# Padding two SBUF tiles so that matmul operands start at multiples of 512 bytes

## The chip, the cores and the metric

One Trainium2 chip, of which the program uses one core. The metric is the device time of one execution in microseconds (us); the figure before is the median of three runs. The engines are called as the profile calls them: PE (TensorE, the matmuls) and PEld (its weight loads, which can run beside its matmuls), DVE (VectorE), ACT (ScalarE), POOL (GpSimd), SP (SyncE, which issues nearly all transfers).

## The reference, cut to what matters

A decoder trunk of two layers on 256 tokens of width 1024, all in float32. Layer 0 mixes tokens by causal averages over 2, 4, 8 and 16 tokens; layer 1 is sparse attention with 16 heads of 64. Behind each mixer stand a gated FFN with a causal convolution of width 3, and a gated embedding:

```python
def conv_ffn(h, w_up, conv_w, conv_b, w_down):      # h 256 x 1024, w_up 1024 x 5632, w_down 2816 x 1024
    u = h @ w_up
    up = jnp.pad(u, ((0, 0), (CONV_W - 1, 0), (0, 0)))
    u = sum(conv_w[j] * up[:, j:j + S] for j in range(CONV_W)) + conv_b
    a, g = u[..., :D_FF], u[..., D_FF:]
    return (jax.nn.silu(g) * a) @ w_down
...
    x = x + conv_ffn(rmsnorm(x, norm_ffn[i]), ffn_up[i], ffn_conv[i], ffn_conv_b[i], ffn_down[i])
    gate = jax.nn.sigmoid(rmsnorm(x, norm_ple[i]) @ ple_gate[i])
    x = x + gate * (p[i] @ ple_proj[i])
```

## The kernel before, in words

The activations lie transposed in SBUF: 128 partitions (features) by 256 tokens, eight such blocks in the tile `x`. Every product is made exact enough by splitting both operands into a rounded part and a rest of type fp32r (`wh`, `wl` for a weight tile, `dh`, `dl` for a down weight, `xs` for both parts of the activations, `ah`, `al` for the FFN's inner activations). `mm3` (line 101) makes three matmuls of 256 columns: high by high, high weight by low activation, low weight by high activation. `mm2` (line 105), used for the up product alone, makes two: the high weight against both parts of the activations side by side (512 columns), then the low weight against the high part (256 columns).

`ahead` (line 137) prepares weights: SP loads 1 MB into `raw`, ACT copies it to `wh`, DVE subtracts to get `wl`, each in two halves (lines 147 and 149). `down_weights` (line 159) does the same for the down weights.

`ffn` (line 325) runs 22 steps per layer. In step i PE makes the up product (`product`, 2 halves by 8 blocks, so 16 calls of `mm2`, line 338), `evac` (line 369) takes it through a copy, an addition, the norm's row, the convolution (lines 377 to 379, on the tile `un`), silu and the split into `ah`, `al`, and `down` (line 389) multiplies the result of two steps before by its down weights: 8 calls of `mm3`, 24 matmuls. The order on PE is: up product of step i, then down product of step i-2. `gates` (line 456) makes the gate's products by `mm3`; `attention_layer` (line 532) makes keys and values from the split `ks` (1280 columns of them by `mm3`), queries from `qs`, scores from `qq` and `kk`, and the output projection from `xo`.

The tiles lie in SBUF in the order in which their pools are opened and their names first used, each at the next multiple of 32 bytes of a partition. This is what the program of the kernel before has (first buffer of each name; all further buffers of the FFN's weights and activations have the same remainder, as their sizes are multiples of 512 bytes):

| tile | byte in the partition | remainder by 512 | role in the matmuls |
|---|---|---|---|
| cols (748 columns, 2,992 bytes) | 16512 | 128 | per-feature constants, identity (48) |
| x | 19520 | 64 | none (input of the splits) |
| identb, maskb (bf16) | 27712, 27968 | 64, 320 | weights, moving operand (attention's mask) |
| raw | 30912 | 192 | none (loaded weights) |
| wh, wl | 55488, 88256 | 192 | weights; moving operand for the values |
| xs, ks, qs, xo, kk (one slot) | 121024 | 192 | moving operand; ks also weights |
| un0, un1, un2 (2 x 258 columns each) | 159360, 161440, 163520 | 128, 160, 192 | none |
| ub, t1, sg | 165600 on | 224 | none |
| ah, al | 173792, 177888 | 224 | moving operand |
| dh, dl | 190176, 198368 | 224 | weights |
| qq, pe (attention) | 159360, 176256 | 128 | weights (scores, transposes) |
| pt, pc, vz (attention) | 212160, 210112, 205504 | 192 | moving operand, weights |

The lines the change touches are these two; each of the three `un` tiles holds two halves of 2 + 256 columns:

```python
    cols = const.tile([P, NCOL], F32, name="cols")                                            # line 171
...
            uns = [fp.tile([P, 2, T + 2], F32, name=f"un{i}", bufs=1) for i in range(3)]      # line 980
            for u in uns:
                G.memset(u[:, :, 0:2], 0.0)
```

and these are the matmuls that the prediction counts:

```python
    def mm3(o, w, x, first, last):
        for i, (a, b) in enumerate(((0, 0), (0, 1), (1, 0))):
            mm(o, w[a], x[b], first and i == 0, last and i == 2)
    def mm2(o, w, x, first, last):
        mm(o, w[0], x, first, False)
        mm(o[:, 1], w[1], x[:, 0], False, last)
```

Of the kernel before, what the change touches and what calls it, by code (L numbers as in the profile page):

```python
# [10 lines left out]
F32 = mybir.dt.float32  # L11
# [7 lines left out]
P = 128  # L19
T = 256  # L20
# [44 lines left out]
def _columns():  # L65
    at, n = {}, 0
    for name, w in (("mix0", 8), ("pscale", 8), ("ffn0", 8), ("ones", 1), ("invf", 1), ("valid", 2),
                    ("ple0", 8), ("kv", 8), ("mix1", 8), ("ffn1", 8), ("ple1", 8),
                    ("final", 8), ("posk", 16), ("posv", 16), ("ident", 128),
                    ("mask", 160), ("conv0", 176), ("conv1", 176)):  # L70
        at[name] = (n, n + w)
        n += w
    return at, n


COLS, NCOL = _columns()


def body(ctx, tc, xt, xT, pT, pos, colsd, band, wpool, wup, wdn, wgate, wproj, wkv, wq, wqg, wout,
# [3 lines left out]
    const = ctx.enter_context(tc.tile_pool(name="const", bufs=1))  # L83
# [84 lines left out]
        dmade[n] = (hi, lo)  # L168


    cols = const.tile([P, NCOL], F32, name="cols")
    c0, c1 = COLS["ones"][0], COLS["conv0"][0]
    x = const.tile([P, KT, T], F32, name="x")
    pool_ctx = ctx.enter_context(ExitStack())
# [255 lines left out]
    def ple(layer):  # L430
        fp = fpool[0]
        pp, wide, wj, ph, pl = {}, [], [], [], []

        def mixin():

            wj[:] = take()
            ahead(3)
            pj = fp.tile([P, 2, T], F32, name="pj", tag="pj", bufs=1)
            nc.sync.dma_start(pj, pT[:, layer])
            ph[:] = [fp.tile([P, 2, T], F32R, name="ph", tag="ph", bufs=1)]  # L440
            pl[:] = [fp.tile([P, 2, T], F32R, name="pl", tag="pl", bufs=1)]
            S.activation(ph[0], pj, AF.Copy, scale=0.5)
            V.scalar_tensor_tensor(pl[0], pj, 0.5, ph[0].bitcast(F32), op0=ALU.mult, op1=ALU.subtract)
            for m in range(PRE):
                inject(m, 5)

        def inject(m, bk, hs=(0, 1)):
            b = bank(bk)
            for h in hs:
                for k in range(2):  # L450
                    mm3(b[:, h], at(wj, slice(None), k, slice((2 * m + h) * P, (2 * m + h + 1) * P)),
                        (ph[0][:, k], pl[0][:, k]), k == 0, k == 1)
            if len(hs) < 2:
                pp[2 * m + hs[0]] = b[:, hs[0]:hs[0] + 1]
                return
            if m % 2 == 0:
                t = fp.tile([P, D], F32, name="pp", tag="draw", bufs=2)
                wide.append(t.rearrange("p (k t) -> p k t", k=4))
            t = wide[m // 2][:, m % 2 * 2:m % 2 * 2 + 2]
            S.copy(t, b)  # L460
            pp[2 * m], pp[2 * m + 1] = t, t[:, 1:]

        return mixin, lambda: gates(layer, inject, pp)
# [499 lines left out]
    def x0ready(k):  # L963
        b = bank((0, 1, 2, 3, 7, 0, 1, 2)[k], (P, T))
        for i in range(2):
            kk = k - k % 2 + i
            mm(b, wpl[:, kk, (k % 2) * P:(k % 2) * P + P], us[:, kk], i == 0, i == 1)
        V.scalar_tensor_tensor(x[:, k], b, col("pscale", k), x[:, k], op0=ALU.mult, op1=ALU.add)

    for layer in range(2):  # L970
        if layer == 1:
            with tc.tile_pool(name="ap", bufs=2) as ap:
                attention_layer(ap)
        if layer == 0:
            for k in range(KT):
                x0ready(k)
            pool_ctx.close()
        with tc.tile_pool(name=f"fp{layer}", bufs=2) as fp:
            fpool[:] = [fp]
            uns = [fp.tile([P, 2, T + 2], F32, name=f"un{i}", bufs=1) for i in range(3)]  # L980
            for u in uns:
                G.memset(u[:, :, 0:2], 0.0)
            mixin, after = ple(layer)
            ffn(layer, mixin)
            after()
# [138 lines left out]
```

## Time and profile before

| | us |
|---|---|
| median of 3 runs (626.06 to 629.3) | 627.59 |
| the profiled execution | 630.54 |
| its span, first to last instruction | 628.8 |
| PE busy | 606.5 (96%), 4134 matmuls |
| PEld busy | 550.7 (88%), 4134 loads |
| DVE busy | 535.1 (85%) |
| ACT busy | 405.7 (65%) |
| mean granted TensorE clock | 0.981 |

[...]

### The profile page before, as it was taken

Reading aid. Unit: us, or ns where it says so; the run is one execution under the profiler, and the core shown is the slowest. Engines: PE = TensorE matmul, PEld = TensorE weight load, DVE = VectorE, ACT = ScalarE, POOL = GpSimd, SP = SyncE. Lnnn points to the kernel's source line nnn. Section 1 sums busy time; section 2 is a strip of 40 time slices with the busy share of each in tenths; the row PEclk is TensorE's granted clock in tenths of the full one; section 3 lists DMA queues with packets and bytes.
Section 4 is the critical chain, followed back from the end, with each engine's and each line's share of the span. In section 5 each row is a group of like instructions: output and inputs, shape, how many; then the busy total and the mean of one; then the engine's idle time right before and its main releaser. Section 6 shows DMA issues by size and latency. Waiting matters only on the chain.

```text
span 628.8 us, 10871 instructions
## 1 busy us (share of the span) xinstructions
PE 606.5 (96%) x4134; PEld 550.7 (88%) x4134; DVE 535.1 (85%) x981; ACT 405.7 (65%) x777; POOL 47.7 (8%) x69
## 2 busy tenths in 40 slices
PE   7999999999999999999889999899999999999995
PEld 7789999999999999999866677699999999999995
DVE  3999999999988889476988974999999998889853
ACT  4868766666676757463675752786666667666743
POOL 1510000000000323000000000500000000000221
PEclk9999999999999999999968999999999999999999
DMA  8775567654554145855532114255654445552001
GB/s 333 292 263 201 176 225 254 239 212 175 169 193 151 52 151 200 323 182 161 172 105 92 67 38 164 86 201 206 241 207 180 173 179 189 201 201 101 1 2 67
DMA packets 24116, 107.32 MB, mean 171 GB/s; under 512 B 3584, under 2 KB 7680, under 8 KB 15744
## 3 DMA queue, kind: packets, MB, share of 16 engines
q1 hardware_dynamic: 23776, 105.58, 47.0%
q10 hardware_dynamic: 288, 1.05, 0.4%
q8 instruction: 32, 0.52, 0.3%
q14 instruction: 20, 0.16, 0.1%
HBM read 101.80 MB, written 1.05 MB: 164 GB/s over the span
## 4 chain that ended last, share of the span: by engine, by line
PE 82%; DVE 4%; ACT 3%; issue 2%; DMA 1%; SPq 1%; POOL 1%; POOLq 0%; DVEq 0%; ACTq 0%
PE bank L99 80%; PE bank L820 2%; ACT wh L147 1%; DMA draw<-in_wdn 1%; DVE wl L149 1%; POOL sqa L276 0%; DVE dl L167 0%; DVE pt L826 0%; SPq L592 0%; ACT pe L782 0%; DMA kk<-kp 0%; DVE nm L770 0%; SPq L701 0%; ACT xs L227 0%; DVE x L739 0%
## 5 line engine op out<-in xcount | busy, mean ns | idle before, releaser
L99 PE MATMUL bank<-xs,wh 128*128 128x512 f32 (+1 forms) x960 | 296.2, 366 | 3.2 <-DVE xs L228 3.0
L99 PE MATMUL bank<-xs,wl 128*128 128x256 f32 x832 | 234.1, 282 | 0.6 <-DVE wl L149 0.6
L99 PEld LDWEIGHTS bank<-xs,wh 128*128 128x128 f32 x960 | 172.5, 189 | 32.6 <-DVE xs L228 5.3
L149 DVE TENSOR_TENSOR wl<-raw,wh 128x1024 fp32r<-128x1024 f32 (+2 forms) x142 | 166.6, 1183 | 20.5 <-ACT wh L147 20.5
L147 ACT CAST wh<-raw 128x1024 fp32r<-128x1024 f32 (+2 forms) x144 | 141.5, 1006 | 38.7 <-PE bank L99 30.0
L99 PEld LDWEIGHTS bank<-xs,wl 128*128 128x128 f32 x832 | 158.2, 190 | 1.4 <-DVE wl L149 1.3
L99 PE MATMUL bank<-al,dh 128*128 128x256 f32 x352 | 99.3, 283 | 0.0
L99 PE MATMUL bank<-ah,dl 128*128 128x256 f32 x352 | 99.1, 283 | 0.0
L99 PE MATMUL bank<-ah,dh 128*128 128x256 f32 x352 | 98.5, 284 | 0.3
L99 PEld LDWEIGHTS bank<-ah,dh 128*128 128x128 f32 x352 | 66.4, 190 | 2.4 <-ACT ah L386 0.7
L99 PEld LDWEIGHTS bank<-al,dh 128*128 128x128 f32 x352 | 67.4, 191 | 0.0
L99 PEld LDWEIGHTS bank<-ah,dl 128*128 128x128 f32 x352 | 67.2, 191 | 0.0
L276 POOL TENSOR_TENSOR sqa<-sqa,sq 128x256 f32<-128x256 f32 x35 | 31.3, 895 | 397.0 <-issue 370.3
L166 ACT CAST dh<-draw 128x1024 fp32r<-128x1024 f32 x44 | 46.2, 1052 | 20.0 <-PE bank L99 16.4
L377 ACT ACTIVATE t<-un,cols 128x256 f32<-128x256 f32 x88 | 52.3, 601 | 10.2 <-DVE un L373 10.0
L371 ACT COPY ub<-bank 128x256 f32<-128x256 f32 x88 | 32.0, 367 | 39.6 <-PE bank L99 39.6
L167 DVE TENSOR_TENSOR dl<-draw,dh 128x1024 fp32r<-128x1024 f32 x44 | 54.1, 1230 | 0.0
L378 DVE SCALAR_TENSOR_TENSOR t<-un,cols,t 128x256 f32<-128x256 f32 x88 | 42.0, 481 | 5.8 <-ACT t L377 5.5
L379 DVE SCALAR_TENSOR_TENSOR t<-un,cols,t 128x256 f32<-128x256 f32 x88 | 41.9, 481 | 1.7
L372 DVE TENSOR_TENSOR ub<-bank,ub 128x256 f32<-128x256 f32 x88 | 36.3, 418 | 0.5
L373 DVE TENSOR_TENSOR un<-ub,rrow 128x256 f32<-128x256 f32 x88 | 36.4, 419 | 0.3
L386 ACT CAST ah<-sg 128x256 fp32r<-128x256 f32 x44 | 17.8, 404 | 17.3 <-DVE sg L383 17.3
(196 smaller groups left out, 861.9 us busy)
## 6 DMA issues: line engine op xcount, KB each, us to landing
raw<-in_wup SPq DMA_DIRECT2D x44, 1024.0 KB, 4.9
draw<-in_wdn SPq DMA_DIRECT2D x44, 512.0 KB, 4.9
raw<-in_wgate SPq DMA_DIRECT2D x8, 1024.0 KB, 4.8
raw<-in_wkv SPq DMA_DIRECT2D x8, 768.0 KB, 4.4
raw<-in_wq SPq DMA_DIRECT2D x4, 1024.0 KB, 5.1
raw<-in_wout SPq DMA_DIRECT2D x4, 1024.0 KB, 4.9
raw<-in_wproj SPq DMA_DIRECT2D x2, 1024.0 KB, 4.8
w<-in_cw SPq DMA_DIRECT2D x2, 1024.0 KB, 6.2
```

The costliest lines, as they stand in the source:

```text
L99: E.matmul(o, w, x, start=first, stop=last, skip_group_check=True)
L147: S.copy(hi[:, sl], raw[:, sl])
L149: e.tensor_tensor(lo[:, sl], raw[:, sl], hi[:, sl].bitcast(F32), op=ALU.subtract)
L166: S.copy(hi, raw)
L167: V.tensor_sub(lo, raw, hi.bitcast(F32))
L276: G.tensor_tensor(acc, acc, t, op=ALU.add)
L371: S.copy(ub, up[i][h][:, 1])
L372: V.tensor_tensor(ub, up[i][h][:, 0], ub, op=ALU.add)
L373: V.tensor_tensor(un[:, h, 2:], ub, row, op=ALU.mult)
L377: S.activation(t1, un[:, h, 2:], AF.Identity, scale=c[2], bias=c[3])
L378: V.scalar_tensor_tensor(t1, un[:, h, 1:T + 1], c[1], t1, op0=ALU.mult, op1=ALU.add)
L379: V.scalar_tensor_tensor(t1, un[:, h, 0:T], c[0], t1, op0=ALU.mult, op1=ALU.add)
```

## The change

```diff
-    cols = const.tile([P, NCOL], F32, name="cols")
+
+    cols = const.tile([P, NCOL + 80], F32, name="cols")[:, :NCOL]
...
-            uns = [fp.tile([P, 2, T + 2], F32, name=f"un{i}", bufs=1) for i in range(3)]
+            uns = [fp.tile([P, 2, T + 24], F32, name=f"un{i}", bufs=1)[:, :, 0:T + 2] for i in range(3)]
```

The padding is never read or written: both tiles are cut back to their old shapes at once. `cols` becomes 3,312 bytes, which takes 3,328 bytes at 32-byte steps in place of 3,008, so everything behind it moves by 320 bytes. Each `un` becomes 2,240 bytes in place of 2,064 (2,080 at 32-byte steps), so what lies behind the three in the FFN's pool moves by 480 more. By this arithmetic `raw`, `wh`, `wl`, `xs` and all tiles of that slot go from remainder 192 to 0; `ub`, `t1`, `sg`, `ah`, `al`, `dh`, `dl` from 224 (+ 320 + 480) to 0; `pt`, `pc`, `vz` from 192 to 0. `x` goes to 384, `qq` and `pe` to 448, `un0` to 448; `cols` stays. No instruction, transfer or wait of the program is written differently apart from these addresses and the pitch of `un`.

## Rows read from the trace of the kernel before

**Rows 1.** The page: span, then busy time, share and instructions of two engines.
```profile
span 628.8 us, 10871 instructions
...
PE 606.5 (96%) x4134; PEld 550.7 (88%) x4134; DVE 535.1 (85%) x981; ACT 405.7 (65%) x777; POOL 47.7 (8%) x69
```

**Rows 2.** Windows: stretch, its length, busy time by engine (instructions), PEclk, DMA share, GB/s.
```profile
core 0: us, PE busy (x) PEld busy (x) DVE busy (x) ACT busy (x) POOL busy (x), PEclk, DMA share, GB/s
...
33.77:201.00 167.23, 167.23 (x1106) 153.77 (x1107) 159.47 (x293) 115.47 (x191) 0.00 (x0) 1.00 0.58 207
201.00:208.70 7.70, 7.55 (x65) 7.35 (x63) 6.30 (x11) 4.81 (x8) 0.00 (x0) 1.00 0.32 103
208.70:276.00 67.30, 67.30 (x519) 65.25 (x520) 50.67 (x79) 41.26 (x78) 14.57 (x21) 1.00 0.50 178
...
310.00:346.00 36.00, 31.26 (x160) 23.15 (x158) 31.33 (x74) 23.63 (x89) 0.00 (x0) 0.76 0.39 116
346.00:386.00 40.00, 37.99 (x271) 29.37 (x273) 33.71 (x77) 23.17 (x75) 0.00 (x0) 1.00 0.18 65
...
406.00:580.60 174.60, 174.60 (x1142) 160.22 (x1143) 160.62 (x282) 119.71 (x194) 2.00 (x2) 0.99 0.52 190
```

**Rows 3.** Timeline of PE, up product: start us, duration us, line, operation.
```profile
20.02 0.39 PE L99 MATMUL bank<-xs,wh 128*128 128x512 f32 x1
20.25 0.28 PE L99 MATMUL bank<-xs,wl 128*128 128x256 f32 x1
...
21.06 0.39 PE L99 MATMUL bank<-xs,wh 128*128 128x512 f32 x1
```

**Rows 4.** Timeline of PE, one down product (sixteen starts apart).
```profile
151.10 0.28 PE L99 MATMUL bank<-ah,dh 128*128 128x256 f32 x1
...
153.02 0.28 PE L99 MATMUL bank<-al,dh 128*128 128x256 f32 x1
```

**Rows 5.** Timeline of DVE and PE: a step's last split, and its first use.
```profile
149.63 0.42 DVE L387 TENSOR_TENSOR al<-sg,ah 128x256 fp32r<-128x256 f32 x1
...
158.94 0.29 PE L99 MATMUL bank<-al,dh 128*128 128x256 f32 x1
```

**Rows 6.** Windows: a piece of attention at the lower clock, columns as in rows 2.
```profile
319.20:319.85 0.65, 0.65 (x5) 0.56 (x4) 0.65 (x3) 0.65 (x2) 0.00 (x0) 0.50 0.00 0
```

**Rows 7.** Timeline of PE in that piece (the first row merges two matmuls).
```profile
319.42 0.63 PE L99 MATMUL bank<-kk,qq 128*128 128x256 f32 x2
...
319.63 0.41 PE L99 MATMUL bank<-kk,qq 128*128 128x256 f32 x1
```

**Rows 8.** Timeline of PE in attention: the causal mask added by a bf16 matmul.
```profile
342.14 0.39 PE L99 MATMUL bank<-maskb,identb 128*128 128x512 bf16 x1
342.37 0.27 PE L820 MATMUL bank<-cols,pe 128*128 128x128 f32 x1
```

**Rows 9.** Timeline of PEld: two weight loads after a wait, no matmul streaming.
```profile
21.71 0.19 PEld L99 LDWEIGHTS bank<-xs,wh 128*128 128x128 f32 x1 [0.46 <-DVE xs L228]
...
21.82 0.19 PEld L99 LDWEIGHTS bank<-xs,wl 128*128 128x128 f32 x1
```

**Rows 10.** Lines of PE: operands, form, count, busy us, mean ns, idle before.
```profile
L99 PE MATMUL bank<-xs,wh 128*128 128x512 f32 (+1 forms) x960 | 296.2, 366 | 3.2 <-DVE xs L228 3.0
L99 PE MATMUL bank<-xs,wl 128*128 128x256 f32 x832 | 234.1, 282 | 0.6 <-DVE wl L149 0.6
L99 PE MATMUL bank<-al,dh 128*128 128x256 f32 x352 | 99.3, 283 | 0.0
...
L99 PE MATMUL bank<-qs,wh 128*128 128x256 f32 x144 | 28.5, 293 | 0.0
L99 PE MATMUL bank<-xo,wh 128*128 128x256 f32 x128 | 25.1, 293 | 0.9 <-DVE x L739 0.7
L99 PE MATMUL bank<-ks,wh 128*128 128x256 f32 x128 | 23.4, 283 | 0.0
...
L99 PE MATMUL bank<-wh,ks 128*128 128x512 f32 x32 | 10.1, 395 | 0.0
...
L99 PE MATMUL bank<-ph,wl 128*128 128x256 f32 x32 | 9.0, 280 | 0.0
```

## The prediction

> **What bounds the kernel now.** I read the page first: PE is busy for 606.5 us of a span of 628.8, DVE for 535.1 [rows 1]. A busy PE is not yet a PE at its peak, so I went to the windows. From 33.77 to 201 and from 406 to 580.6, the two FFN layers, PE has no idle time at all, at a granted clock of 1.00 and 0.99; the same holds from 208.7 to 276, the gates and the keys and values. DVE is busy there for 159.47 of 167.23 and 160.62 of 174.6 us [rows 2]. Those 409 us are the matmul stream's alone. The timeline shows what the stream costs: in the up product a pair of 512 and 256 columns takes (21.06 - 20.02) / 3 = 0.3467 us, of which the first matmul takes 0.23 and the second 0.117 [rows 3]; in the down product sixteen matmuls of 256 columns, each with new weights, take 153.02 - 151.10 = 1.92 us, 0.120 each [rows 4]. A step of an FFN layer is therefore 16 x 0.3467 + 24 x 0.120 = 8.43 us.
>
> **What the stream loses.** [...] All these operands lie at remainder 192 or 224 by 512. From there a row of 2,048 bytes touches five blocks of 512 bytes, and a row of 1,024 bytes three. [...]
>
> **The change, part by part.** It adds no instruction, transfer or wait; it moves addresses. *Matmuls.* At remainder 0 the row of 2,048 bytes touches four blocks, that of 1,024 two, the weight row one. [...] A pair goes from 346.7 to 340.0 ns and a single matmul with its load from 120.0 to 113.3: 6.67 ns each. The counts are in the lines [rows 10]:
> the up pairs, 2 layers x 22 x 16 = 704, give 704 x 6.67 ns = 4.7 us;
> the down matmuls, three groups of 352, give 7.0 us;
> the other streams of 256 columns are the gates' 960 - 704 = 256 with wh and 832 - 704 = 128 with wl, the keys' 128 + 64, the queries' 144 + 72, the projection's 128 + 64 (wl has half as many as wh in `mm3`) and the embedding's 3 x 32: 1,080, so 7.2 us;
> the values' 32 + 16 matmuls of 512 columns give 0.2 us at 3.3 ns.
> Together 19.1 us.
>
> What of this doesn't reach the end: from 201 to 208.7 PE is out of work at times (7.55 of 7.70 busy [rows 2]), as the last step's evacuation ends there, and the two layers' 65 matmuls each, 0.9 us, only lengthen that wait. In attention PE waits for exponentials and maxima (31.26 busy of 36 us from 310, 37.99 of 40 from 346), so I count nothing of the projection's 1.3 us and of some 0.5 us of late queries. The first pairs, up to 33, wait for splits: 0.3 us. That leaves 19.1 - 0.9 - 1.8 - 0.3 = 16.1 us.
>
> Would another engine become late? A step's last DVE result is written at 149.63 + 0.42 = 150.05, and first used at 158.94 [rows 5], 8.9 us ahead. In layer 0 DVE has the backlog of the start and the rope tables to make up; its whole idle time is 167.23 - 159.47 = 7.8 us, and PE would ask it to finish 22 x 0.267 = 5.9 us sooner (16 x 6.67 + 24 x 6.67 ns = 0.267 us a step). That fits, narrowly; in layer 1 (14 us idle) easily.
>
> *DVE, ACT and transfers.* Their tiles move too. No row shows an operation of theirs at another remainder with all else equal, so the bound is from both sides: DVE and ACT are off the path where they gain, and where they lose they have the 8.9 us. Zero. *Shapes.* `un` has a wider pitch between its halves; each instruction takes one half, so nothing changes. *Reuse.* `ub` and what lies behind it in the FFN's pool shift by 480 bytes against the earlier pools. A few first uses may wait for other old tiles; the matmul stream from 33.77 on hides all but the first, so I take zero, bounded by the 0.15 us that PE idles from 201 to 208.7 [rows 2].
>
> The sum stands against the profiled execution: 630.5 - 16.1 = 614.4 us, of which 1.7 lie around the span. That execution is 2.95 us above the median of 627.59; against the median it is **611.5 us**.
>
> **Both ends of the unknown price.** The trace has no matmul of this type at remainder 0. At one end the address changes nothing, 0 us. [...]
>
> **Rivals.** *(A) Blocks matter for both ports*, as summed: 611.5, between 606 and 617 as more or less of the attention's and the gates' part counts. [...] Chance 0.45.
> *(B) Only the moving rows gain.* The loads stay at 0.120 us and hide what the single matmuls win; pairs gain, as 0.117 leaves room. 704 x 6.67 ns + 0.2 - 0.3 = 4.6 us, so 623. The two loads [rows 9] speak for it. Chance 0.12.
> *(C) The change doesn't do what it says: no address matters.* [...] Then 627.6, within 2 us. [...] Chance 0.30. [...]
> *(D) Slower, through the clock.* If PE gets ahead of ACT and DVE in attention, or a wait shifts there, a second stretch of lower clock may come. From 310 to 346 the clock is 0.76, with PE idle for 4.7 us of 36: 36 x 0.24 = 8.6 us of full clock lost. The place would be 346 to 386, where the clock is 1.00 and PE idles 2 us of 40 [rows 2]. It decides only if the matmuls gain under 5 us: 627.6 + 8.6 = 636. With (A) it would give 620. Against it: PE idles there for 2 us now [rows 2], and a matmul stream 2% shorter adds little to that. Chance 0.07.
> More than (A), down to 627.6 - 40 = 587 (47 us less what doesn't reach the end), would need DVE to be done far more than 7.8 us sooner in layer 0; it has 0.06.
>
> **How the numbers follow.** 0.5% is 3.1 us, about what a measurement of this kernel can tell from no change. Faster by more than that are (A), (B) and the rest: 0.63. Within it (C): 0.30. Slower (D): 0.07. The range for 8 times in 10 takes in (A), (B) and (C): 605 to 629; it leaves out (D), most of the 0.06 and thin tails.
>
> **What would show it.** Right: in the changed kernel's timeline the pair of the up product takes 0.340 us, the down matmuls start 0.113 apart, the step is 8.16 us, and PE is still full in both FFN layers. Wrong at the loads (B): 0.340, but 0.120. Wrong altogether (C): 0.347 and 0.120. A PE with gaps in layer 0 would mean that DVE became the bound; a second stretch at 0.50 in attention is (D).

## The result, and the profile after

The change makes the kernel slower: 632.91 us (median of 7 runs, 630.83 to 636.11) against 627.99 of the kernel before (7 runs on the same chip, 626.06 to 629.3). The ratio is 1.0069, with a 95% interval of 1.0041 to 1.0097. The profiled execution of after took 633.14 us.

The page of after, its span, the busy times, and the lines of the up product's and one of the down product's matmuls:

```profile
span 631.3 us, 10871 instructions
...
PE 609.1 (96%) x4134; PEld 549.7 (87%) x4134; DVE 535.9 (85%) x981; ACT 405.6 (64%) x777; POOL 47.7 (8%) x69
...
L99 PE MATMUL bank<-xs,wh 128*128 128x512 f32 (+1 forms) x960 | 300.7, 371 | 2.1 <-DVE xs L229 1.9
...
L99 PE MATMUL bank<-al,dh 128*128 128x256 f32 x352 | 99.2, 283 | 0.0
```

The instructions are as many as before, and on every engine they come in the same order. PE is busy for 2.6 us more [rows 1], and the line that holds the up product's 512-column matmuls for 4.5 us more (300.7 for 296.2 [rows 10]), while the down product's line stands where it stood (99.2 for 99.3). The windows of after show the rest:

```profile
34.00:201.00 167.00, 167.00 (x1095) 152.27 (x1095) 158.18 (x288) 114.31 (x189) 0.00 (x0) 1.00 0.58 206
...
310.00:346.00 36.00, 29.86 (x180) 21.62 (x178) 33.77 (x78) 25.85 (x94) 0.00 (x0) 0.91 0.43 122
...
406.00:583.00 177.00, 177.00 (x1137) 161.09 (x1138) 159.78 (x281) 119.90 (x194) 1.62 (x1) 0.98 0.52 185
```

PE is full in both FFN layers, as before, at a clock of 1.00 and 0.98 (before 1.00 and 0.99 [rows 2]). So no wait was added; the stream itself got longer. The timeline of PE in after shows by how much: three up pairs, and sixteen streams of the down product (a **stream** is one matmul with its weight load).

```profile
52.94 0.40 PE L99 MATMUL bank<-xs,wh 128*128 128x512 f32 x1
53.17 0.28 PE L99 MATMUL bank<-xs,wl 128*128 128x256 f32 x1
53.29 0.40 PE L99 MATMUL bank<-xs,wh 128*128 128x512 f32 x1
53.52 0.28 PE L99 MATMUL bank<-xs,wl 128*128 128x256 f32 x1
53.64 0.40 PE L99 MATMUL bank<-xs,wh 128*128 128x512 f32 x1
53.88 0.28 PE L99 MATMUL bank<-xs,wl 128*128 128x256 f32 x1
54.00 0.40 PE L99 MATMUL bank<-xs,wh 128*128 128x512 f32 x1
...
57.88 0.28 PE L99 MATMUL bank<-ah,dh 128*128 128x256 f32 x1
...
59.80 0.28 PE L99 MATMUL bank<-al,dh 128*128 128x256 f32 x1
...
60.76 0.40 PE L99 MATMUL bank<-xs,wh 128*128 128x512 f32 x1
```

A matmul is counted here from its start to that of the next: the first row lists 0.40 us, but the next matmul starts 0.23 us later. Three pairs take 54.00 - 52.94 = 1.06 us, 0.3533 each, for 1.04 us and 0.3467 before [rows 3]; sixteen down streams take 1.92 us in both [rows 4]. The three pairs are no longer alike: 0.35, 0.35 and 0.36 us, and then the same again. In the text below, the **quick rhythm** is that of before (347 ns a pair, every pair alike), the **slow rhythm** any that needs 353. Three pairs read to 0.01 us are a coarse sample: over many pairs the means are 347.2 and 353.0 ns (table below), so a pair takes 5.8 ns longer.

The last up pair of layer 0, the first, the 33rd and the last of layer 1, in the timeline of before and then of after:

```profile
200.63 0.39 PE L99 MATMUL bank<-xs,wh 128*128 128x512 f32 x1
...
397.80 0.50 PE L99 MATMUL bank<-xs,wh 128*128 128x512 f32 x1 [0.29 <-DVE xs L228]
...
414.80 0.39 PE L99 MATMUL bank<-xs,wh 128*128 128x512 f32 x1
...
580.23 0.39 PE L99 MATMUL bank<-xs,wh 128*128 128x512 f32 x1
```
```profile
202.47 0.40 PE L99 MATMUL bank<-xs,wh 128*128 128x512 f32 x1
...
397.11 0.50 PE L99 MATMUL bank<-xs,wh 128*128 128x512 f32 x1 [0.32 <-DVE xs L229]
...
415.50 0.39 PE L99 MATMUL bank<-xs,wh 128*128 128x512 f32 x1
...
582.69 0.40 PE L99 MATMUL bank<-xs,wh 128*128 128x512 f32 x1
```

The up pairs of layer 0 end 1.84 us later. Those of layer 1 take 582.69 - 397.11 - (580.23 - 397.80) = 3.15 us longer, but only 582.69 - 415.50 - (580.23 - 414.80) = 1.76 us of that lie in the pairs from the 33rd on. The other 1.39 us lie in the first 32, where PE still waits at times and the granted clock was lower in after (0.66 for 0.83); the windows of before and then of after:

```profile
404.00:414.00 10.00, 8.43 (x43) 7.17 (x42) 9.26 (x15) 7.98 (x13) 3.92 (x3) 0.83 0.50 178
```
```profile
404.00:414.00 10.00, 9.23 (x37) 7.95 (x38) 7.55 (x13) 7.73 (x12) 3.21 (x3) 0.66 0.61 216
```

So the pairs at a granted clock of 1.00 account for 1.84 + 1.76 = 3.6 us of the 4.92 between the medians. The interval of the ratio (0.41% to 0.97%) is 2.6 to 6.1 us and holds both; the rest is not attributed. Nor do the two profiled executions differ by 4.92: in between, after took 2.5 us less (397.11 - 202.47 = 194.64 for 197.17), with a higher clock in attention (0.91 from 310 to 346, for 0.76 [rows 2]). Neither piece of clock is the change's doing: p_after_row2 (below), with all tiles where after has them, had 0.76 from 310 to 346 and 1.00 from 404 to 414, and p_before_row2 had 0.91 from 310 to 346. In 27 runs the kernel before itself took between 626.07 and 632.89 us, so single times below decide nothing; the verdicts rest on the pair in the trace, and on the kernels that were timed ten times or more.

### The profile page after: what moved, and what is told of

The parts are those of the page before. It is cut to its first block, busy times and chain, and to the rows that moved or that the text cites. A ratio compares the mean times of both kernels' runs of the same rounds, so it can differ in the third digit from the quotient of the medians.

```text
span 631.3 us, 10871 instructions
## 1 busy us (share of the span) xinstructions
PE 609.1 (96%) x4134; PEld 549.7 (87%) x4134; DVE 535.9 (85%) x981; ACT 405.6 (64%) x777; POOL 47.7 (8%) x69
## 4 chain that ended last, share of the span: by engine, by line
PE 81%; DVE 4%; ACT 3%; issue 2%; DMA 1%; POOL 1%; SPq 1%; POOLq 0%; DVEq 0%; ACTq 0%
PE bank L99 80%; PE bank L821 1%; POOL sqa L277 1%; ACT wh L147 1%; DMA draw<-in_wdn 1%; DVE nm L771 1%; DVE wl L149 1%; SPq L593 0%; DMA kk<-kp 0%; SPq L702 0%; DMA qq<-qp 0%; DVE dl L167 0%; DVE x L740 0%; DVE pt L827 0%; ACT xs L228 0%
## 5 line engine op out<-in xcount | busy, mean ns | idle before, releaser
L99 PE MATMUL bank<-xs,wh 128*128 128x512 f32 (+1 forms) x960 | 300.7, 371 | 2.1 <-DVE xs L229 1.9
L99 PE MATMUL bank<-al,dh 128*128 128x256 f32 x352 | 99.2, 283 | 0.0
L99 PE MATMUL bank<-ah,dl 128*128 128x256 f32 x352 | 99.2, 283 | 0.0
L99 PE MATMUL bank<-qs,wh 128*128 128x256 f32 x144 | 28.6, 294 | 0.0
```

The source lines that it names most:

```text
L99: E.matmul(o, w, x, start=first, stop=last, skip_group_check=True)
```

## The experiments

**First four: which padding.** Theory 1 was the forecast's with its sign turned: an up operand at remainder 0 is worse than at 192. Theory 2 looked at the work tiles of VectorE and ScalarE.

```diff
e1_cols_only
+cols = const.tile([P, NCOL + 80], F32, name="cols")[:, :NCOL]
e2_un_only
+uns = [fp.tile([P, 2, T + 24], F32, name=f"un{i}", bufs=1)[:, :, 0:T + 2] for i in range(3)]
e3_xs_moved (constants and un as before)
+xpad = xp.tile([P, 80], F32, name="xpad", bufs=1)
+G.memset(xpad[:, 0:1], 0.0)
e4_weights_moved (constants padded as in e1, un as before)
+xpad = xp.tile([P, 48], F32, name="xpad", bufs=1)
+G.memset(xpad[:, 0:1], 0.0)
```

> Only cols is padded (80 columns): wh, wl and xs go to remainder 0 by 512, the FFN's work tiles to 32. Theory 1 (the up product's own operands at remainder 0 are what slows it): the pair of 512 and 256 columns takes 0.3533 us as in the changed kernel, 704 x 6.67 ns = 4.7 us, so about 632.7 us. Theory 2 (the evacuation's tiles at remainder 0 collide with PE's reads): the pair stays at 0.3467 us and the time at 628.

> Only the three un tiles are padded: wh, wl and xs stay at remainder 192, the FFN's work tiles (ub to dl) go from 224 to 192. Theory 1 (the up product's own operands): pair 0.3467 us, time 628, no change. Theory 2 (the evacuation's tiles' place, or the wider pitch of un): pair above 0.35 us and time up to 632.7.

> xs alone goes to remainder 0, wh and wl stay at 192. If the moving row's remainder slows the pair: 0.3533 us. If the weight rows' remainder does, or only both together at 0: 0.3467 us. The distance between xs and the weights changes for the first time, so any other value means that the distance counts.

> wh and wl go to remainder 0, xs stays at 192. If the weight rows' remainder slows the pair: 0.3533 us. If the moving row's remainder does, or only both together at 0: 0.3467 us. Any other value means that the distance between the two counts.

Measured: e1 628.6 us (ratio 0.9991, interval 0.997 to 1.0012), pairs of 347.2 ns. e2 633.61 us (ratio 1.0064, 1.0043 to 1.0084), pairs of 353.0 ns. e3 and e4, one run each: 630.91 and 632.43 us, pairs of 353.1 and 353.2 ns. Theory 1 falls twice. With the up operands at remainder 0 (e1) nothing changes, and with them left at 192 (e2) the whole loss is there. In e2 not one operand of the up product has another address than before; the tiles that moved are `un` and those behind it in the FFN's pool: `ub`, `t1`, `sg`, and the down product's rows `ah`, `al` and weights `dh`, `dl`, from remainder 224 to 192. e3 and e4, slow as well, show that moving `xs` against `wh` costs too: from `xs` on, e3 has every tile where e1 has it, and only `wh`, `wl` and what lies ahead of them stand 320 bytes lower.

**Next four: a phase, a pitch, or a place.** In the slow rhythm of after the pairs differ in threes (0.35, 0.35 and 0.36 us), though their instructions are alike and PE waits for nothing, as if something carried on from pair to pair. So theory 3 was that PE falls into one or the other by chance where it resumes after a wait. The p kernels shift that moment by a wider product; the a kernels move addresses in other ways.

```diff
p_before_row2 (p_after_row2: the same in the kernel after)
-    mm(b[:, 256 + i * P:256 + (i + 1) * P], ones, dg[:, i], True, True)
+    lo = i * (P - 2)
+    mm(b[:, 256 + lo:256 + (i + 1) * P], ones, dg.rearrange("p a b -> p (a b)")[:, lo:(i + 1) * P], True, True)
a_un8
+uns = [fp.tile([P, 2, T + 10], F32, name=f"un{i}", bufs=1)[:, :, 0:T + 2] for i in range(3)]
a_cols8
+cols = const.tile([P, NCOL + 8], F32, name="cols")[:, :NCOL]
```

> The kernel before, with the second half of each norm row's product (the last products that TensorE runs before it enters the up product of a layer, at 34 and at 411 us) two columns wider, 130 for 128, two of them computed twice. Nothing else differs: same addresses, same order. Theory 3 (the rhythm of the up pairs is a phase that TensorE's own stream falls into where it resumes, and that carries itself on): the entry comes about 3 ns later, by the 128 columns' 436 ns of four passes, so the phase may fall otherwise; the mean pair of at least one layer goes from 347 to some 350 to 353 ns, and the kernel by up to +5 us. Theory 4 (the place or pitch of the FFN's work tiles sets the speed of the pair): 347 ns in both layers, the time as before.

> The kernel after, with the same two columns more in each norm row's second product. Theory 3: the phase may fall otherwise, and at least one layer's mean pair goes from 353 to about 347 ns, worth 2.3 us for each layer that does. Theory 4: 353 ns in both layers, the time as after, 633 us.

> The kernel before, with un wider by 8 columns only (pitch 266 for 258): the tiles behind it, the operands of the down product among them, lie at remainder 416 of 512, an odd multiple of 32 as before (224); those of the change lie at multiples of 64. Theory 4a (the down operands' and work tiles' remainder of 64 sets the rhythm): 347 ns, the time as before. Theory 4b (any other pitch of un): 353 ns, about 633 us. Theory 3: either, with no rule in the address; the two layers and the two programs may even differ.

> The kernel before, with the constants wider by 8 columns only: every tile behind lies 32 bytes on, un keeps its pitch, the up product's operands lie at remainder 224 and the down product's at 256, a multiple of 64. Theory 4a (remainder of 64): 353 ns, about 633 us. Theory 4b (pitch of un): 347 ns, the time as before. Theory 3: either.

Measured, one run each: 627.09, 634.09, 627.16 and 627.34 us, with pairs of 347.2, 353.0, 346.8 and 347.6 ns in layer 0. Neither p kernel changed its rhythm behind the first down product, so the moment of entry doesn't decide that. Theory 4b falls for the pitch of 266 (a_un8), theory 4a with a_cols8: its down operands lie at 256, a multiple of 64, and it is quick. But a_cols8 told where the choice is made. The timeline of PE at layer 0's start, after and then a_cols8: the first stream after the wait, the first of the down product, the up pairs behind it and the next down product.

```profile
34.26 0.36 PE L99 MATMUL bank<-xs,wl 128*128 128x256 f32 x1
...
41.88 0.40 PE L99 MATMUL bank<-ah,dh 128*128 128x256 f32 x2
...
45.46 0.40 PE L99 MATMUL bank<-xs,wh 128*128 128x512 f32 x1
...
49.35 0.28 PE L99 MATMUL bank<-ah,dh 128*128 128x256 f32 x1
```
```profile
34.20 0.36 PE L99 MATMUL bank<-xs,wl 128*128 128x256 f32 x1
...
41.82 0.28 PE L99 MATMUL bank<-ah,dh 128*128 128x256 f32 x1
...
45.39 0.39 PE L99 MATMUL bank<-xs,wh 128*128 128x512 f32 x1
...
49.21 0.28 PE L99 MATMUL bank<-ah,dh 128*128 128x256 f32 x1
```

Up to the first down product both take 7.62 us, the slow rhythm. Behind it, eleven pairs take 3.89 us in after and 3.82 in a_cols8. The down block hands on the rhythm.

**Three that part `un` from what lies behind it.**

```diff
b_un_place: places as in e2, pitch 258 (three tiles of 560 words, of which 516 are used)
b_behind_only: un as before; the last of the three tiles has 636 words
b_un_only_back: un as in e2 (pitch 280); the last of the three tiles has 568 words
+for i, n in enumerate((560, 560, 560)):          # (516, 516, 636); (560, 560, 568) with pitch 280
+    u = fp.tile([P, n], F32, name=f"un{i}", bufs=1)[:, :516]
+    uns.append(u.rearrange("p (a b) -> p a b", a=2)[:, :, :T + 2])
```

> Every tile lies where it lies with only un padded (un and all behind it moved, the down product's operands at remainder 192), but un keeps its pitch of 258 inside the wider tile. Theory 5 (where the down product's operands and the other tiles behind un lie decides which rhythm the down block hands on to the next up pairs): 353 ns, about 633 us. Theory 4b (the pitch of un): 347 ns, the time as before. Theory 3 (any phase, no rule in the address): either.

> The three un tiles lie as before, place and pitch; only what lies behind them moves by 480 bytes (the last un tile is 120 words longer, unused), so that the down product's operands lie at remainder 192 as with only un padded. Theory 5: 353 ns, about 633 us. Theory 4b: 347 ns. Theory 6 (VectorE's and ScalarE's accesses to un itself, by its place, disturb the phase): 347 ns. Theory 3: either.

> The reverse: un lies as with un padded, place and pitch (280), and what lies behind is moved 32 bytes further, so that it has the remainders of before (224). Theory 5: 347 ns, the time as before. Theory 4b and theory 6: 353 ns, about 633 us. Theory 3: either.

Measured, one run each: 631.66, 631.86 and 629.31 us, pairs of 353.0, 352.6 and 347.2 ns in layer 0. Theory 5 holds in all three. The timeline of b_behind_only, at the same four points:

```profile
34.18 0.36 PE L99 MATMUL bank<-xs,wl 128*128 128x256 f32 x1
...
41.68 0.34 PE L99 MATMUL bank<-ah,dh 128*128 128x256 f32 x1
...
45.31 0.40 PE L99 MATMUL bank<-xs,wh 128*128 128x512 f32 x1
...
49.20 0.28 PE L99 MATMUL bank<-ah,dh 128*128 128x256 f32 x1
```

It is the reverse of a_cols8: quick up to the first down product (7.50 us), slow behind it (3.89).

**Four for the rule.** All runs so far with `xs` and `wh` at one remainder fit one sentence: slow where the down product's operands have the up product's remainder, quick where they are an odd multiple of 32 bytes away.

```diff
c_both_224: constants 8 columns wider, last un tile 636 words
c_up0_down64: constants 80 columns wider, last un tile 524 words
c_dw192_a224: un as before; ahead of the first draw of a layer (120 words; in c_dw224_a192 8, and the last un tile 636)
+    if n % NP == 0:
+        fpool[0].tile([P, 120], F32, name="dpad", tag="dpad", bufs=1)
     raw = fpool[0].tile([P, D], F32, name="draw", tag="draw", bufs=2)
```

> Constants wider by 8 columns, and the tiles behind un moved by 480 bytes: the operands of the up product and of the down product all lie at remainder 224 of 512. Theory 7 (the slow rhythm comes where both products' operands have the same remainder, the quick one where they differ by an odd multiple of 32): 353 ns, about +4 us to the kernel before. Theory 8 (the absolute remainder of the down operands decides; 224 was quick, 192 and 0 slow): 347 ns, the time as before.

> Constants wider by 80 columns (the up product's operands at remainder 0) and the tiles behind un 32 bytes further than with that alone: the down product's operands at remainder 64. Theory 7a (the difference counts by 64 bytes): 0 and 64 are alike, 353 ns, about +4 us. Theory 7b (only the same remainder of 512 is slow): 347 ns, the time as before.

> The tiles behind un as with only un padded, but the down product's weights moved 32 bytes further by a small unused tile ahead of them: weights at remainder 224, moving rows at 192, up operands at 192. The unused tile gives the whole program another order of instructions, so it is compared with c_dw192_a224 alone, which has the same order. If the weights' place decides: quick here (347 ns), slow there (353). If the moving rows' place decides: slow here, quick there, the two some 4 us apart. If neither alone: both alike.

> The reverse in the same order of instructions: the down product's weights at remainder 192, its moving rows at 224, up operands at 192. If the weights' place decides: slow here (353 ns), quick in c_dw224_a192. If the moving rows' place decides: quick here (347 ns), slow there. If neither alone: both alike.

Measured, one run each: 633.87, 632.0, 632.26 and 626.77 us. The first two are slow (352.6 and 353.2 ns), so with `xs` and `wh` at one remainder the difference decides, and 0 and 64 count alike: theory 7a. One thing in the expectations was wrong: the unused tile only renumbers the tiles, and every engine's order is the old one, so the two c_dw kernels compare with all others (e3 and e4 too, but for one memset on POOL). Their timelines, c_dw224_a192 and then c_dw192_a224: the start of sixteen pairs, of the down product behind them, and of the next pairs.

```profile
69.20 0.40 PE L99 MATMUL bank<-xs,wh 128*128 128x512 f32 x1
...
74.86 0.28 PE L99 MATMUL bank<-ah,dh 128*128 128x256 f32 x1
...
77.70 0.40 PE L99 MATMUL bank<-xs,wh 128*128 128x512 f32 x1
```
```profile
68.96 0.39 PE L99 MATMUL bank<-xs,wh 128*128 128x512 f32 x1
...
74.51 0.28 PE L99 MATMUL bank<-ah,dh 128*128 128x256 f32 x1
...
77.34 0.39 PE L99 MATMUL bank<-xs,wh 128*128 128x512 f32 x1
```

Sixteen pairs take 5.66 and 5.55 us: the place of the moving rows decides, not that of the weights. And in both the 24 down streams take 2.84 and 2.83 us, where after takes 60.76 - 57.88 = 2.88: a second effect, where the rows and weights of the down product lie an odd multiple of 32 apart.

**Last three: the rule as a time.**

```diff
d_after_plus32: the kernel after, and the last un tile 568 words for 560
d_dw192_a224: c_dw192_a224 again
d_odd_all: 8 words ahead of draw, and ahead of xs
+    xp.tile([P, 8], F32, name="xpad", tag="xpad", bufs=1)
```

> The whole change, and the tiles behind un 32 bytes further: the up product's operands at remainder 0, the down product's at 32. Theory 7a (agreement by 64 between the two products is what costs): the quick rhythm, 347 ns a pair, ratio to the kernel before 1.000, within 0.3%. Rival (the change costs by something else, un's place and pitch or the constants): 1.007.

> c_dw192_a224 again, timed: up operands and the down product's weights at remainder 192, its moving rows at 224. By its trace, quick pairs from the third step on (347 ns) and down streams of 117.9 for 120.0 ns, which times 1056 is 2.2 us: ratio to the kernel before 0.995 to 0.998. Rival (its one time of 626.8 was the draw of a lucky phase or of the clock in attention): 1.000 and more.

> Two unused tiles of 32 bytes, one ahead of xs and one ahead of the down product's weights: the up product's weights at 192 and rows at 224, the down product's rows at 256 and weights at 288 (32): weights and rows of each product differ by 32. Theory 9 (a product whose weights and rows differ by an odd multiple of 32 is quicker, 2.1 ns for each stream as seen in the down product): pairs of some 343 ns, down streams of 118 ns, together 2.8 and 2.2 us, about 0.992 of the kernel before. Rival (the pairs keep the quick rhythm only where their weights and rows agree, as e3 and e4 suggest): 353 ns, which times 704 is +4.4 us, less 2.2 us for the down streams, 1.003.

Measured against the kernel before (628.87 us, 27 runs): d_after_plus32 628.77 us, ratio 1.0 (0.9978 to 1.0022); d_dw192_a224 627.69, ratio 0.9972 (0.9946 to 0.9997); d_odd_all 625.36, ratio 0.9935 (0.9911 to 0.996). Thirty-two bytes take the whole loss of the change away. d_odd_all beats both kernels, though half of theory 9 failed: the up pair went to 346.9 ns, not 343. The timeline of d_odd_all, sixteen pairs and the down product behind them:

```profile
51.87 0.40 PE L99 MATMUL bank<-xs,wh 128*128 128x512 f32 x1
...
57.42 0.28 PE L99 MATMUL bank<-ah,dh 128*128 128x256 f32 x1
...
60.25 0.40 PE L99 MATMUL bank<-xs,wh 128*128 128x512 f32 x1
```

5.55 us for the pairs, 2.83 for the down streams. The down streams are worth 1056 x 2 ns = 2.1 us; other products gain as well. Nine streams of the keys' product in d_odd_all and in before:

```profile
247.78 0.40 PE L99 MATMUL bank<-ks,wh 128*128 128x256 f32 x2
...
248.82 0.40 PE L99 MATMUL bank<-ks,wh 128*128 128x256 f32 x2
```
```profile
249.85 0.40 PE L99 MATMUL bank<-ks,wh 128*128 128x256 f32 x2
...
250.93 0.63 PE L99 MATMUL bank<-wh,ks 128*128 128x512 f32 x2
```

1.04 us there, 1.08 here.

**All placements together.** Remainder by 512 of the up product's weights and rows and of the down product's rows and weights; means in layer 0 over the pairs and streams whose records are complete (ns):

```
kernel                        wh   xs   ah   dh    pair   down
before                       192  192  224  224   347.2  120.2
p_before_row2                192  192  224  224   347.2  120.2
b_un_only_back               192  192  224  224   347.2  120.1
e1_cols_only                   0    0   32   32   347.2  120.2
d_after_plus32                 0    0   32   32   347.2  120.1
a_cols8                      224  224  256  256   347.6  120.0
a_un8                        192  192  416  416   346.8  119.8
after, p_after_row2            0    0    0    0   353.0  120.0
e2_un_only, b_un_place       192  192  192  192   353.0  120.0
b_behind_only                192  192  192  192   352.6  120.1
c_both_224                   224  224  224  224   352.6  120.2
c_up0_down64                   0    0   64   64   353.2  119.2
c_dw224_a192                 192  192  192  224   353.3  118.5
c_dw192_a224, d_dw192_a224   192  192  224  192   347.5  118.1
d_odd_all                    192  224  256  288   346.9  118.3
e3_xs_moved                  192    0   32   32   353.1  119.7
e4_weights_moved               0  192  224  224   353.2  119.9
```

(d_dw192_a224 by itself: 347.9 and 117.9.) In every row but the last two, the pair is quick where `ah` and `xs` differ by an odd multiple of 32, and slow where they differ by a multiple of 64. d_odd_all, whose `ah` agrees with `wh` by 64 and not with `xs`, speaks for `xs` as the one that counts, but it is a single placement. In e3 and e4 the rule would have given the quick rhythm and didn't; there `xs` and `wh` differ by 192 by remainder, which no other row has, and the pairs have rhythms of their own. By 64 bytes e3 has all the remainders of e1 and is slow (353.1 ns) where e1 is quick (347.2), so the remainder by 64 is not the whole rule. What such a difference does was not followed up.

## Why the prediction was wrong

**What bounds the kernel** was right: PE's stream alone, full in both layers before and after, so that a longer pair reached the end of its layer (1.84 us over the 352 pairs of layer 0). That the pair moved by nearly the 6.67 ns of the forecast is luck: its mean went from 347.2 to 353.0 ns, 5.8 ns the other way, by something that the forecast doesn't hold.

**The step that failed** is the gain of 6.67 ns for each pair and each single stream, 3.3 for the values' matmuls. No run shows this term: it was the author's estimate, which took the blocks of 512 bytes that an operand touches for what costs. e1 puts the up operands where they touch 4 and 2 blocks for 5 and 3, and the pair takes 347.2 ns, as before; e2 leaves them at 5 and 3, and it takes 353.0. The down streams stay at 120.0 to 120.2 ns at remainders 192, 224, 0 and 32 alike. So the absolute place by 512 bytes is worth nothing here. Of the terms of the sum, the 4.7 us of the up pairs came out as a loss of some 3.6 us, the 7.0 us of the down streams as nothing; of the 7.2 us of the other streams the keys' product shows nothing either: nine of its streams take 1.08 us in after (251.82 to 252.90) as in before. Two rows of before were the better guide: two weight loads at remainder 192 start 0.11 us apart [rows 9], which the estimate has for remainder 0 alone (113.3 ns), and the mask's 512 columns of bf16 take 0.23 us from remainder 320 [rows 8], as the up product's do from 192 [rows 3]. What counted is how operands lie to each other, and the change, by bringing the rows of both products to one remainder, made an alignment that cost 5.8 ns a pair.

**The term taken as zero** that carried the result stands under *Reuse*: "`ub` and what lies behind it in the FFN's pool shift by 480 bytes". It was weighed for waits alone, with 0.15 us as the bound. b_behind_only makes this shift alone and gets the slow rhythm of the change (352.6 ns). The bound was wrong because an address was thought to matter only for its own instruction's time. Here the down product's streams take as long as ever (120.1 ns for 120.2), and the pairs behind them, whose addresses didn't move, pay. The zero for *DVE, ACT and transfers* held: PE waits for nothing new.

**The rivals.** (A) and (B) fall with the 6.67 ns. (C), that no address matters, had it right for the absolute remainder (e1, d_after_plus32: no difference within 0.3%) and wrong for the relative one. With the up operands at remainder 0 in both, e1 takes the time of before (0.9991) and after does not (1.0069). (D) had the right sign by the wrong way: the lower clock in attention came out shorter in the profile of after (0.91 for 0.76 [rows 2]), and its length changes from one execution to the next (0.76 in p_after_row2, 0.91 in p_before_row2). No rival held a pair that grows; the bound on an unknown price was drawn from 0 to 47 us of gain, though the trace had nothing that excluded a loss. No run shows the 47 us either, an estimate of the author's: the largest gain measured is 3.5 us (d_odd_all, 625.36 for 628.87).

## What to carry to other kernels

Padding operands to a round multiple was no good by itself here (0.9991 in e1, 1.0069 in after); in a saturated matmul stream look at the distance between operands. Here it paid to keep the moving rows of products that follow each other an odd multiple of 32 bytes apart, as they lie in the kernel before; the change undid that (0.69%). To set the weights and rows of one product so as well, by a few unused words ahead of a tile, gave 0.65% against the kernel before (d_odd_all): the down and keys' streams gained by it (118.3 ns for 120.2, and nine in 1.04 us for 1.08), the up pair didn't (346.9 ns for 347.2). It has to be tried and read in the starts of the matmuls, pair by pair, since the rule failed for two placements of this kernel (e3, e4) and no other kernel was tried.

## What was not expected of the hardware

Two rhythms of the same PE instructions at the same addresses, 347 and 353 ns a pair. c_dw192_a224 and d_dw192_a224 are one kernel; the timelines from the first stream after the wait of layer 0 to the first of the down product, in that order:

```profile
34.33 0.36 PE L99 MATMUL bank<-xs,wl 128*128 128x256 f32 x1
...
41.81 0.35 PE L99 MATMUL bank<-ah,dh 128*128 128x256 f32 x1
```
```profile
34.23 0.36 PE L99 MATMUL bank<-xs,wl 128*128 128x256 f32 x1
...
41.85 0.29 PE L99 MATMUL bank<-ah,dh 128*128 128x256 f32 x1
```

7.48 us, the quick rhythm, and 7.62, the slow one: in this first stretch the rhythm differs from one execution to the next, so there theory 3 has it right. Behind the first down product the two executions agree: eleven pairs take 3.87 us (45.42 to 49.29 in c_dw192_a224) and the next sixteen 5.64, both slow; then sixteen take 5.56, and 5.55 from there on, quick. So in these runs a rhythm carried on through a stretch of pairs (21 pairs of the slow one in after and in a_cols8 alike, 7.62 us with the stream ahead of them), and the down blocks kept or changed it, by the place of their rows, not always in one step. Moving the entry by two columns (p kernels) didn't matter beyond the first stretch. After and a_cols8 agree in 43 starts and differ with the first streams of the down block, while `ub`, `t1` and `sg` are in use throughout; that points to the place of `ah` and `al`, but no run moved these two without the other work tiles. What in the chip makes the rhythm is open: the runs show the rule, not its cause.

How far a pair could still fall was not shown: over all placements it takes 346.8 (a_un8) to 353.3 ns (c_dw224_a192).
